# Queries and keys turned by VectorE squares and GpSimd copies; the turned softmax weights stored from ScalarE's queue

## The chip, the cores and the metric

The kernel runs on one core of a Trainium2 chip, in one launch. The metric is the device time of that launch in microseconds (us). A core has TensorE (PE, matrix products, with a weight load PEld of its own in the profile), VectorE (DVE), ScalarE (ACT), GpSimd (POOL) and SyncE (SP), which work through their own instructions in order and wait for each other through semaphores. Transfers are started by an instruction on SP's, ACT's or POOL's queue and run on 16 DMA engines.

## The reference

A decoder trunk of two layers on 256 tokens of 2048 channels, all in float32. Layer one mixes tokens with gated linear attention, layer two with block attention whose block of 256 holds the whole sequence, so that each query sees its own block, causally, with a bias by distance. Each is followed by a gated ConvFFN. The part that the change touches is the second mixer, here for one batch and one block:

```python
q = (rms_norm(x, norm_w) @ w_q).reshape(B, S, H, Dh)          # H = 16 heads of Dh = 128
q = rms_norm(q, q_norm_w) * Dh ** -0.5
k = rms_norm((rms_norm(x, kv_norm) @ w_k).reshape(B, S, H, Dh), k_norm_w)
v = (rms_norm(x, kv_norm) @ w_v).reshape(B, S, H, Dh)
s = einsum('qhd,khd->hqk', q, k) + bias_table[:, rel_bucket(dist)]
p = softmax(where(dist >= 0, s, -inf))
o = einsum('hqk,khd->qhd', p, v)
h = h + o.reshape(B, S, H * Dh) @ w_out
```

## The kernel before

**Weights and steps.** Every weight matrix is streamed from DRAM once, in chunks of 128 x 2048 (1 MB) on SP's queue into three buffers (`wraw`). A chunk is two halves of 1024 columns. ScalarE casts each half to the high part `whi` (L144), VectorE subtracts to get the remainder `wlo` (L146); four buffers of each exist. TensorE multiplies high by high, low by high and high by low parts, which is nearly float32. The Python call `step()` hands out one half and advances a counter `cur`; `after(n, job)` puts a job n steps later, so lags are counted in weight halves. `tc.issue_after(ws.high.ins)` and `ws.low.ins` keep an instruction behind the latest cast on ScalarE, or remainder on VectorE. The final order on each engine is set by a scheduler when the kernel is built; tiles come out of pools, above all 32 slots of 4 KB per partition (`slot`), two PSUM banks for small products (`bank`) and three PSUM accumulators of two banks (`acc`).

**The stage around the change.** `gemm_tok` (L366/L368 belong to its sibling `gemm`, L381/L384 to it) makes four groups of queries, four of keys, four of values, each group four heads of 128 channels with tokens on partitions, in 8 steps of 12 matmuls of 512 columns. Behind each query or key group:

- `head_norm` squares and copies the accumulator out on ScalarE (L989, L990), sums the squares per head on VectorE (L992, L993), raises them to -1/2 on GpSimd (`rr`, L995) and scales the rows on VectorE (L997).
- `features`, two jobs 3 and 4 steps later, turns tokens x channels into channels x tokens: four TensorE transposes of 128 x 128 into a PSUM bank `tr` (L1005), two ScalarE copies out (L1008, L1010) and a VectorE remainder (L1011).
- for keys, `softmax` 5 to 8 steps later: four matmuls per head into `s` (L1021, L1023), bias, minimum, exponential, sum and scaling (L1030 to L1036).
- `turn`, 7 to 10 steps later: VectorE transposes 32 x 32 squares within partitions (L1045); four GpSimd-queue stores to DRAM (L1048) and one load back (L1049) exchange the squares, so that keys lie on partitions.
- `weights`, 15 to 18 steps later: high, low and plain parts on ScalarE and VectorE (L406, L407, L1061).

`values` follows each value group by 1 and 2 steps: eight matmuls per head (L460 to L463) and a split into `ox`, which is what the output projection (`project`, L366/L368) multiplies. `bias_rows` builds the bias rows with a one-hot matmul (L972) and four loads on GpSimd's queue. In the same stage `make_ahead` forms sums of the last weight matrix's blocks on VectorE (L329, L330) and parks them in DRAM (`tsum`, 1 MB each, GpSimd's queue, L339).

`square` (L700) is a helper of the ConvFFN already: after a VectorE transpose of 32 x 32 squares (L722) sixteen GpSimd copies (L705) move the squares between groups of 32 partitions. `turn_h` stores turned squares to DRAM (`hscr`, L874) on SP's queue, 32 KB each.

Of the kernel before, what the change touches and what calls it, by code (L numbers as in the profile page):

```python
# [8 lines left out]
F32 = mybir.dt.float32  # L9
F32R = mybir.dt.float32r  # L10
I32 = mybir.dt.int32
AF = mybir.ActivationFunctionType
OP = mybir.AluOpType
# [5 lines left out]
S = 256  # L19
# [139 lines left out]
def trunk(ctx: ExitStack, tc: tile.TileContext, xT, cst, msk, w1p, w2a, w_k, w_qa, w_v2, w_v, w_g, w_go,  # L159
          w_up0, w_dn0, w_kk, w_kv, w_mq, w_mo, w_up1, w_dn1, rel, onehot, out):  # L160
    nc = tc.nc
    V, A, T = nc.vector, nc.scalar, nc.tensor
# [11 lines left out]
    def slot(shape, dt, name):  # L174
        return big.tile(shape, dt, name=name, tag="slot")

    def temp(name, shape=(128, 2, S), dt=F32):
        return tmp.tile(list(shape), dt, name=name, tag="temp")

    def bank(name, shape):  # L180
        return mis_ps.tile(list(shape), F32, name=name, tag="bank")
# [6 lines left out]
    for layer, todo in enumerate(ahead):  # L188
        t = dram.tile([len(todo), 128, 2048], F32, name=f"tsum{layer}")
# [15 lines left out]
    h = [hs[p // 2][:, p % 2] for p in range(NP)]  # L205
# [4 lines left out]
    kqw = keep.tile([128, 1], F32, name="kqw")  # L210
# [36 lines left out]
    ident = mk[:, 0:128]  # L247
# [73 lines left out]
    def after(steps, job):  # L321
        later.append((cur[0] + steps, job))
# [21 lines left out]
    def after_high():  # L344
        return tc.issue_after(ws.high.ins)

    def after_low():
        return tc.issue_after(ws.low.ins)
# [40 lines left out]
    def rows(xs):  # L389
        return lambda kt: xs[kt // 2][:, kt % 2, :]  # L390

    def both(ps, name):
        t = temp(name)
        A.copy(t, ps[:, :, S:])
        V.tensor_add(t, t, ps[:, :, :S])
        return t
# [8 lines left out]
    def split(dst_hi, dst_lo, src):  # L405
        A.copy(dst_hi, src)  # L406
        V.tensor_sub(dst_lo, src, dst_hi.bitcast(F32))  # L407
# [129 lines left out]
    for hd in range(GH):  # L537
        ps = gemm(xs, KT)
        rstd = nrm.rstd
        k = both(ps, "k")  # L540
        V.tensor_mul(k, k, bc(rstd))
        b = bcum[hd]
        d = small.tile([128, 2, 4], F32, name="dec", bufs=4)
# [63 lines left out]
    for hd in range(GH):  # L607
        ps = gemm(xs, KT)
        q = both(ps, "q")
# [11 lines left out]
    for hd in range(GH):  # L621
        for c in range(2):
            ps = gemm(xs, KT)
            g = both(ps, "g")
# [75 lines left out]
    def square(y, x):  # L700

        for m in range(4):
            xs_ = x[32 * m:32 * m + 32].rearrange("a t (n c b) -> a n t c b", c=4, b=32)
            for c in range(4):
                nc.gpsimd.tensor_copy(y[32 * c:32 * c + 32, :, :, 32 * m:32 * m + 32], xs_[:, :, :, c])  # L705
# [279 lines left out]
    def head_norm(ps, name):  # L985
        t_, sq = slot([128, 2, 512], F32, name), slot([128, 2, 512], F32, "hsq")
        for t in range(2):
            r = n_q.col[:, t:t + 1]
            A.activation(sq[:, t, :], ps[:, t, :], AF.Square, scale=r)  # L989
            A.activation(t_[:, t, :], ps[:, t, :], AF.Copy, scale=r)  # L990
        ss = small.tile([128, 8], F32, name="ss")
        V.tensor_reduce(ss, sq.rearrange("p t (h d) -> p (t h) d", d=128), axis=AX.X, op=OP.add)  # L992
        V.tensor_scalar(ss, ss, 1.0 / 128, EPS, op0=OP.mult, op1=OP.add)  # L993
        rr = small.tile([128, 8], F32, name="rr")
        nc.gpsimd.tensor_tensor(rr, ss, mhalf, op=OP.pow)  # L995
        u = t_.rearrange("p t (h d) -> p (t h) d", d=128)
        V.tensor_mul(u, u, rr[:, :, None].to_broadcast([128, 8, 128]))  # L997
        return t_

    def features(t_, c, f, scale, c0):  # L1000

        tp = bank("tr", (128, 2, S))
        for i in range(2):
            for t in range(2):
                T.transpose(tp[:, i, 128 * t:128 * t + 128],  # L1005
                            t_[:, t, (2 * c + i) * 128:(2 * c + i + 1) * 128], ident)
        whole, halves_ = f[0][:, 2 * c:2 * c + 2, :], f[1][c]
        A.activation(whole, tp[:, :, :128], AF.Copy, scale=scale)  # L1008
        hi, lo = halves_[:, :, 0, :], halves_[:, :, 1, :]
        A.activation(hi, tp[:, :, c0:], AF.Copy, scale=scale)  # L1010
        V.scalar_tensor_tensor(lo, tp[:, :, c0:], scale, hi.bitcast(F32), op0=OP.mult, op1=OP.subtract)  # L1011

    qf, kf, ox = [], [], []
    pts = [None] * MH
    p0s, p1s = [], []

    def softmax(hd):
        (q0, q1), (k0, k1) = qf[hd // 4], kf[hd // 4]
        q1, k1 = q1[hd // 2 % 2][:, hd % 2], k1[hd // 2 % 2][:, hd % 2]
        sp = bank("s", (128, 384))  # L1020
        T.matmul(sp[:, 0:128], q0[:, hd % 4, :], k0[:, hd % 4, :], start=True, stop=True)  # L1021
        for i, (a, b) in enumerate(((0, 0), (0, 1), (1, 0))):
            T.matmul(sp[:, 128:384], q1[:, a, :], k1[:, b, :], start=i == 0, stop=i == 2)  # L1023
        s = temp("s", (128, 384))
        st = small.tile([128, 4], F32, name="st")
        bt = bias[hd // 4][:, hd % 4, :]
        for t, (c0, c1) in enumerate(((0, 128), (128, 384))):
            n = c1 - c0
            rev = bass.AP(tensor=bt.tensor, offset=bt.offset + n - 1, ap=[bt.ap[0], [-1, n]])
            V.tensor_tensor_reduce(s[:, c0:c1], sp[:, c0:c1], rev, -1.0, 3.0e38, OP.add, OP.min,  # L1030
                                   st[:, t:t + 1])
            A.activation(s[:, c0:c1], s[:, c0:c1], AF.Exp, bias=st[:, t:t + 1], scale=-1.0,
                         accum_out=st[:, 2 + t:3 + t])
        V.reciprocal(st[:, 2:4], st[:, 2:4])
        for t, (c0, c1) in enumerate(((0, 128), (128, 384))):
            V.tensor_scalar(s[:, c0:c1], s[:, c0:c1], st[:, 2 + t:3 + t], None, op0=OP.mult)  # L1036
        pts[hd] = s

    turned = dram.tile([MH, 12, 32, 128], F32, name="turned")

    def turn(hd):

        t = slot([128, 2, 384], F32, "pT")
        with tc.issue_after(ws.low.ins):
            V.transpose(t[:, 0], pts[hd])  # L1045
        to = turned[hd].rearrange("f b (m a) -> m b f a", a=32)
        for m in range(4):
            nc.gpsimd.dma_start(to[m], t[32 * m:32 * m + 32, 0].rearrange("b (f a) -> b f a", a=32))  # L1048
        nc.gpsimd.dma_start(t[:, 1].rearrange("k (j q) -> k j q", j=3),  # L1049
                            turned[hd].rearrange("(j f) b q -> (f b) j q", f=4))  # L1050
        pts[hd] = t[:, 1]

    def weights(hd):
        tp = pts[hd]
        if hd % 8 == 0:
            p1s.append(slot([128, 8, 128], F32, "p1"))
        if hd % 2 == 0:
            p0s.append(slot([128, 2, 2, S], F32R, "p0"))
        with tc.issue_after(ws.high.ins):
            split(p0s[-1][:, hd % 2, 0], p0s[-1][:, hd % 2, 1], tp[:, :256])  # L1060
            A.copy(p1s[-1][:, hd % 8], tp[:, 256:])  # L1061
# [17 lines left out]
    for g in range(4):  # L1079
        ps = gemm_tok(xs)  # L1080
        t_ = head_norm(ps, "q")
        if g % 2 == 0:
            q8 = slot([128, 8, 128], F32, "q0")
        q1 = slot([128, 4, 2, 128], F32R, "q1")
        f = (q8[:, g % 2 * 4:g % 2 * 4 + 4], (q1[:, 0:2], q1[:, 2:4]))
        qf.append(f)
        for c in range(2):
            after(3 + c, lambda t_=t_, c=c, f=f: features(t_, c, f, 1.0, 128))
    xs = rows(xkv)
    for g in range(4):  # L1090
        ps = gemm_tok(xs)
        t_ = head_norm(ps, "k")
        if g % 2 == 0:
            k8 = slot([128, 8, 128], F32, "k0")
        f = (k8[:, g % 2 * 4:g % 2 * 4 + 4], [slot([128, 2, 2, S], F32R, f"k1{c}") for c in range(2)])
        kf.append(f)
        for c in range(2):
            after(3 + c, lambda t_=t_, c=c, f=f: features(t_, c, f, kqw, 0))
        for i in range(4):
            after(5 + i, lambda i=i, g=g: softmax(4 * g + i))  # L1100
            after(7 + i, lambda i=i, g=g: turn(4 * g + i))
            after(15 + i, lambda i=i, g=g: weights(4 * g + i))
    for g in range(4):
        ps = gemm_tok(xs)
        if g % 2 == 0:
# [120 lines left out]
```

## Time and profile before

| | us |
|---|---|
| median of 3 runs | 2176.6 (2175.9 to 2176.62) |
| profiled execution | 2175.2 |
| its span, first to last instruction | 2173.4 |
| TensorE's granted clock | 1.000 |
| queries' and keys' transposes on TensorE | 1129.2 to 1310.8 |
| softmax, first score to last weight | 1223 to 1354 |
| last values to the projection | 1384.9 |

Times in the profile count from the span's start. A row of a group names line, engine, operation, output<-input, shapes and count, then its busy time and mean, then the idle time of the engine just before and what ended it. TensorE's matmuls are pipelined, so the duration of one is a latency, and its price is the distance between starts. ScalarE's and VectorE's queues show a DMA start as its own row (`ACTq`, `SPq`), not as busy time; on GpSimd it counts as busy.

### The profile page before, as it was taken

What the parts mean: (1) busy time and instruction counts of PE and PEld (TensorE: products, weight loads), DVE (VectorE), ACT (ScalarE), POOL (GpSimd) and SP (SyncE); (2) the same over time, 40 slices, a digit from 0 to 9 for tenths busy, and PEclk for the clock granted to TensorE, in tenths of its full rate; (3) what the DMA queues carried; (4) which work ended last, traced back from release to release, by engine and by line L of the source; (5) the groups of instructions that cost most, each with busy time, mean ns of one, the idle gap of its engine ahead of it and who ended that gap; (6) DMA issues with size and microseconds to landing.
All of it is one profiled execution on the core that took longest, in us unless ns stands there. A gap on an engine that the chain in (4) does not pass through costs nothing.

```text
span 2173.4 us, 29230 instructions
## 1 busy us (share of the span) xinstructions
PE 2165.5 (100%) x10224; PEld 1815.1 (84%) x10224; DVE 1829.8 (84%) x2531; ACT 1311.9 (60%) x1849; POOL 659.4 (30%) x925
## 2 busy tenths in 40 slices
PE   9999999999999999999999999999999999999999
PEld 7889888888888888887888888888888888888887
DVE  7676877699999897977978787677999999979898
ACT  6655655456565655766756666445565656567575
POOL 0000000264656464300001343003655565542000
PEclk9999999999999999999999999999999999999999
DMA  7575778777778785887967788677787878759896
GB/s 289 209 289 178 263 263 321 287 263 285 273 281 313 275 311 191 329 329 259 366 245 293 275 299 294 228 285 276 284 302 275 310 284 290 293 191 349 325 358 251
DMA packets 113526, 613.01 MB, mean 282 GB/s; under 512 B 29361, under 2 KB 29889, under 8 KB 49634
## 3 DMA queue, kind: packets, MB, share of 16 engines
q1 hardware_dynamic: 94610, 523.75, 66.5%
q0 software_dynamic: 18048, 86.60, 10.5%
q8 instruction: 80, 1.31, 0.2%
q10 hardware_dynamic: 720, 0.79, 0.1%
q14 instruction: 68, 0.56, 0.1%
HBM read 535.31 MB, written 75.78 MB: 281 GB/s over the span
## 4 chain that ended last, share of the span: by engine, by line
PE 98%; DMA 2%; DVE 0%; ACT 0%; issue 0%; ACTq 0%; DVEq 0%; SPq 0%
PE acc L381 40%; PE acc L384 20%; PE acc L803 13%; PE acc L366 11%; PE acc L368 6%; PE p L803 5%; DMA wraw<-w_dn 1%; PE sT L577 0%; DMA sums<-tsum 0%; DMA ahead<-tsum 0%; PE tr L1005 0%; PE s L1023 0%; DVE wlo L146 0%; DMA h<-xT 0%; PE z L483 0%; PE o L463 0%
## 5 line engine op out<-in xcount | busy, mean ns | idle before, releaser
L146 DVE TENSOR_TENSOR wlo<-wraw,whi 128x1024 fp32r<-128x1024 f32 (+1 forms) x788 | 954.3, 1221 | 266.6 <-ACT whi L144 179.8
L144 ACT CAST whi<-wraw 128x1024 fp32r<-128x1024 f32 (+1 forms) x788 | 797.1, 1018 | 611.9 <-PE acc L381 361.8
L381 PE MATMUL acc<-whi,xw 128*128 128x512 f32 x3328 | 825.5, 389 | 0.6 <-DVE xw L261 0.6
L381 PEld LDWEIGHTS acc<-whi,xw 128*128 128x128 f32 x3328 | 623.5, 188 | 130.4 <-issue 1.1
L705 POOL COPY up<-uT 32x256 f32<-32x256 f32 x704 | 520.9, 740 | 310.5 <-DVE uT L722 240.7
L384 PE MATMUL acc<-wlo,xw 128*128 128x512 f32 x1664 | 445.9, 389 | 0.0
L384 PEld LDWEIGHTS acc<-wlo,xw 128*128 128x128 f32 x1664 | 312.1, 188 | 65.0 <-DVE wlo L146 0.3
L339 POOL DMA_DIRECT2D tsum<-ahead x58 | 31.6, 545 | 549.3 <-DVE ahead L330 511.7
L803 PE MATMUL acc<-whi,hid 128*128 128x512 f32 x588 | 168.1, 390 | 1.3 <-ACT whi L144 1.3
L146 DVE TENSOR_TENSOR wlo<-ahead,whi 128x1024 fp32r<-128x1024 f32 x98 | 120.4, 1235 | 19.0 <-ACT whi L144 12.2
L803 PEld LDWEIGHTS acc<-whi,hid 128*128 128x128 f32 x588 | 109.8, 188 | 24.7 <-ACT whi L144 2.3
L381 PE MATMUL acc<-whi,xkv 128*128 128x512 f32 x512 | 129.9, 391 | 0.0
L144 ACT CAST whi<-ahead 128x1024 fp32r<-128x1024 f32 x98 | 101.9, 1054 | 42.9 <-PE p L803 18.5
L366 PE MATMUL acc<-xw,whi 128*128 128x512 f32 x512 | 124.5, 392 | 0.0
L803 PE MATMUL p<-whi,hid 128*128 128x512 f32 x356 | 111.5, 389 | 0.0
L381 PEld LDWEIGHTS acc<-whi,xkv 128*128 128x128 f32 x512 | 95.1, 188 | 18.9
L366 PEld LDWEIGHTS acc<-xw,whi 128*128 128x128 f32 x512 | 93.6, 188 | 17.7
L803 PE MATMUL acc<-whi,comb 128*128 128x512 f32 x348 | 101.3, 390 | 0.7 <-ACT whi L144 0.7
L803 PE MATMUL acc<-wlo,hid 128*128 128x512 f32 x294 | 96.3, 390 | 0.0
L735 ACT ACTIVATE au<-up,cs 128x256 f32<-128x256 f32 x176 | 96.1, 595 | 0.0
L742 DVE SCALAR_TENSOR_TENSOR au<-up,cs,au 128x254 f32<-128x254 f32 x176 | 90.2, 543 | 0.0
L740 DVE SCALAR_TENSOR_TENSOR au<-up,cs,au 128x255 f32<-128x255 f32 x176 | 89.2, 543 | 0.2
(266 smaller groups left out, 2355.3 us busy)
## 6 DMA issues: line engine op xcount, KB each, us to landing
wraw<-w_up SPq DMA_DIRECT2D x176, 1024.0 KB, 5.5
ahead<-w_dn SPq DMA_DIRECT2D x58, 1024.0 KB, 8.9
tsum<-ahead POOLq DMA_DIRECT2D x58, 1024.0 KB, 8.8
ahead<-tsum SPq DMA_DIRECT2D x49, 1024.0 KB, 6.9
wraw<-w_dn SPq DMA_DIRECT2D x58, 768.0 KB, 6.3
wraw<-w_dn SPq DMA_DIRECT2D x30, 1024.0 KB, 6.7
wraw<-w_g SPq DMA_DIRECT2D x16, 1024.0 KB, 4.9
wraw<-w_go SPq DMA_DIRECT2D x16, 1024.0 KB, 6.2
```

What stands on the lines that cost most here:

```text
L144: self.high = nc.scalar.copy(hi[:, a:b], src[:, a:b])
L146: self.low = nc.vector.tensor_sub(lo[:, a:b], src[:, a:b], hi[:, a:b].bitcast(F32))
L339: after(8, lambda: nc.gpsimd.dma_start(parked[layer][at], t))
L366: T.matmul(ps[:, b, :], two[i][0][:, c:c + 128], xs(kt), start=kt == 0, stop=False)
L368: T.matmul(ps[:, b, :S], two[i][1][:, c:c + 128], xs(kt)[:, :S], start=False, stop=kt == kts - 1)
L381: T.matmul(ps[:, t, :], xs(kt)[:, x0 + 128 * t:x0 + 128 * t + 128], hi[:, c:c + 512], start=kt == 0 and x0 == 0, stop=False)
L384: T.matmul(ps[:, t, :], xs(kt)[:, 128 * t:128 * t + 128], lo[:, c:c + 512], start=False, stop=kt == KT - 1)
L705: nc.gpsimd.tensor_copy(y[32 * c:32 * c + 32, :, :, 32 * m:32 * m + 32], xs_[:, :, :, c])
L735: A.activation(au[:, i, :], t[:, i, :], AF.Identity, bias=col(cb + n), scale=col(cw + 2 * 2 * FT + n))
L740: V.scalar_tensor_tensor(au[:, i, 1:], t[:, i, :S - 1], col(cw + 2 * FT + n), au[:, i, 1:], op0=OP.mult, op1=OP.add)
L742: V.scalar_tensor_tensor(au[:, i, 2:], t[:, i, :S - 2], col(cw + n), au[:, i, 2:], op0=OP.mult, op1=OP.add)
L803: T.matmul(p[n], x[xi], w[wi][:, 512 * f:512 * f + 512], start=n not in begun, stop=left[n] == 0)
```

## The change

The four transposes per half group on TensorE and their PSUM bank go. One job per group, 6 steps after it, scales the rows (behind the latest remainder), transposes the 32 x 32 squares of all four heads with one VectorE instruction of 128 x 1024, and lets `square` move them with 16 GpSimd copies into `y`. Two further jobs, 7 and 8 steps after that, read `y` where the PSUM bank was read. The lags of `softmax`, `turn` and `weights` grow from 5, 7, 15 to 17, 19, 30. In `turn`, the four stores move to a job one step later and from GpSimd's queue to ScalarE's, behind the latest cast; the load back stays on GpSimd's queue, in that same job. Line numbers behind the change differ: in the changed kernel the scaling is L1004, the transpose L1005, the copies out L1013, L1014 and L1016, the stores L1059, the load L1060.

```diff
@@ -993,22 +993,30 @@
-        u = t_.rearrange("p t (h d) -> p (t h) d", d=128)
-        V.tensor_mul(u, u, rr[:, :, None].to_broadcast([128, 8, 128]))
-        return t_
-
-    def features(t_, c, f, scale, c0):
-
-        tp = bank("tr", (128, 2, S))
-        for i in range(2):
-            for t in range(2):
-                T.transpose(tp[:, i, 128 * t:128 * t + 128],
-                            t_[:, t, (2 * c + i) * 128:(2 * c + i + 1) * 128], ident)
-        whole, halves_ = f[0][:, 2 * c:2 * c + 2, :], f[1][c]
-        A.activation(whole, tp[:, :, :128], AF.Copy, scale=scale)
-        hi, lo = halves_[:, :, 0, :], halves_[:, :, 1, :]
-        A.activation(hi, tp[:, :, c0:], AF.Copy, scale=scale)
-        V.scalar_tensor_tensor(lo, tp[:, :, c0:], scale, hi.bitcast(F32), op0=OP.mult, op1=OP.subtract)
+        return t_, rr
+
+    def features(t_, f, scale, c0, lag):
+
+        x, y = slot([128, 2, 512], F32, "tr"), slot([128, 4, S], F32, "tr")
+        u, rr = t_
+        u = u.rearrange("p t (h d) -> p (t h) d", d=128)
+        with after_low():
+            V.tensor_mul(u, u, rr[:, :, None].to_broadcast([128, 8, 128]))
+        V.transpose(x.rearrange("p t c -> p (t c)"), t_[0].rearrange("p t c -> p (t c)"))
+        square(y.rearrange("p n (t s) -> p n t s", t=2), x)
+
+        def out_(c):
+            u = y[:, 2 * c:2 * c + 2]
+            whole, halves_ = f[0][:, 2 * c:2 * c + 2, :], f[1][c]
+            hi, lo = halves_[:, :, 0, :], halves_[:, :, 1, :]
+            with after_high():
+                A.activation(whole, u[:, :, :128], AF.Copy, scale=scale)
+                A.activation(hi, u[:, :, c0:], AF.Copy, scale=scale)
+            with after_low():
+                V.scalar_tensor_tensor(lo, u[:, :, c0:], scale, hi.bitcast(F32), op0=OP.mult, op1=OP.subtract)
+
+        for c in range(2):
+            after(lag[c], lambda c=c: out_(c))
@@ -1044,11 +1052,16 @@
         to = turned[hd].rearrange("f b (m a) -> m b f a", a=32)
-        for m in range(4):
-            nc.gpsimd.dma_start(to[m], t[32 * m:32 * m + 32, 0].rearrange("b (f a) -> b f a", a=32))
-        nc.gpsimd.dma_start(t[:, 1].rearrange("k (j q) -> k j q", j=3),
-                            turned[hd].rearrange("(j f) b q -> (f b) j q", f=4))
-        pts[hd] = t[:, 1]
+
+        def store():
+            for m in range(4):
+                with after_high():
+                    A.dma_start(to[m], t[32 * m:32 * m + 32, 0].rearrange("b (f a) -> b f a", a=32))
+            nc.gpsimd.dma_start(t[:, 1].rearrange("k (j q) -> k j q", j=3),
+                                turned[hd].rearrange("(j f) b q -> (f b) j q", f=4))
+            pts[hd] = t[:, 1]
+
+        after(1, store)
@@ -1084,8 +1097,7 @@
-        for c in range(2):
-            after(3 + c, lambda t_=t_, c=c, f=f: features(t_, c, f, 1.0, 128))
+        after(6, lambda t_=t_, f=f: features(t_, f, 1.0, 128, (7, 8)))
@@ -1094,12 +1106,11 @@
-        for c in range(2):
-            after(3 + c, lambda t_=t_, c=c, f=f: features(t_, c, f, kqw, 0))
+        after(6, lambda t_=t_, f=f: features(t_, f, kqw, 0, (7, 8)))
         for i in range(4):
-            after(5 + i, lambda i=i, g=g: softmax(4 * g + i))
-            after(7 + i, lambda i=i, g=g: turn(4 * g + i))
-            after(15 + i, lambda i=i, g=g: weights(4 * g + i))
+            after(17 + i, lambda i=i, g=g: softmax(4 * g + i))
+            after(19 + i, lambda i=i, g=g: turn(4 * g + i))
+            after(30 + i, lambda i=i, g=g: weights(4 * g + i))
```

## The prediction

> **What bounds the kernel now.** I read the page first, then the queries and keys' stage alone: its stretches, its waits, its PE timeline.
>
> ```profile
> PE 2165.5 (100%) x10224; PEld 1815.1 (84%) x10224; DVE 1829.8 (84%) x2531; ACT 1311.9 (60%) x1849; POOL 659.4 (30%) x925
> PE 98%; DMA 2%; DVE 0%; ACT 0%; issue 0%; ACTq 0%; DVEq 0%; SPq 0%
> ...
> 1222.00:1332.00 110.00, 110.00 (x545) 93.06 (x544) 94.79 (x208) 72.78 (x152) 54.47 (x79) 1.00 0.83 290
> 700.00:800.00 100.00, 100.00 (x442) 82.83 (x442) 93.80 (x132) 60.31 (x86) 55.50 (x79) 1.00 0.76 276
> ...
> ACT whi L144 <- PE acc L381: 95.4, 68, 4.4
> ```
>
> The first two rows are the page's busy times and its chain of waits: TensorE is busy for the whole span, and the chain that ends last is TensorE for 98%. The next two are stretches (after the length: PE, PEld, DVE, ACT, POOL busy, granted clock, DMA share): 1222 to 1332 is where the softmax runs, 700 to 800 lies in the first ConvFFN, whose up-projection is turned already in the way that the change brings in. TensorE has no gap in either. The last is the longest of the waits between 1080 and 1400 us: ScalarE's weight cast waits 95.4 us for TensorE to give a weight buffer back; no wait of TensorE for a cast stands in that list. So every TensorE instruction taken out of this stage should come off the end, as long as nothing that replaces it makes TensorE wait.
>
> **What is removed.** 64 transposes of 128x128.
>
> ```profile
> L1005 PE MATMUL tr<-mk,q x32: 270/272/328, 1129.2 to 1195.4; 128*128 128x128 f32 x32
> ...
> L1005 PE MATMUL tr<-mk,k x32: 270/272/273, 1216.2 to 1310.8; 128*128 128x128 f32 x32
> ```
> ```profile
> 1157.96 1.07 PE L384 MATMUL acc<-wlo,xw 128*128 128x512 f32 x4
> 1158.87 1.98 PE L381 MATMUL acc<-whi,xw 128*128 128x512 f32 x8
> 1160.69 1.03 PE L1005 MATMUL tr<-mk,q 128*128 128x128 f32 x8
> 1161.48 1.17 PE L384 MATMUL acc<-wlo,xw 128*128 128x512 f32 x4
> 1162.48 1.98 PE L381 MATMUL acc<-whi,xw 128*128 128x512 f32 x8
> ```
> ```profile
> by line: PE acc L381 61.4%; PE acc L384 30.8%; PE tr L1005 3.6%; PE s L1023 2.5%; PE s L1021 1.5%; PE biasrow L972 0.4%
> ```
>
> The 272 ns are a latency; the price is the distance between starts. Eight L381 matmuls take 1160.69 - 1158.87 = 1.82 us, four L384 matmuls 1158.87 - 1157.96 = 0.91 us; so a weight half (one "step") is 2.73 us. Eight transposes take 1161.48 - 1160.69 = 0.79 us, and the four L384 matmuls behind them 1.00 instead of 0.91. That is 0.88 us per eight, 7.0 us for 64. The chain over 1120 to 1320 us, which holds all 64, says the same: 3.6% of 200 us is 7.2. I take 7.0.
>
> **What is added on VectorE and GpSimd.** Per group of four heads (eight groups) one 128x1024 square transpose on VectorE and 16 copies on GpSimd.
>
> ```profile
> L705 POOL COPY up<-uT 32x256 f32<-32x256 f32 x704 | 520.9, 740 | 310.5 <-DVE uT L722 240.7 <-PE acc L384 22.3 <-issue 20.0
> ...
> L722 DVE STREAM_TRANSPOSE uT<-up 128x512 f32<-128x512 f32 x88 | 58.3, 693 | 0.0
> ...
> L1045 DVE STREAM_TRANSPOSE pT<-s 128x384 f32<-128x384 f32 x16 | 9.0, 571 | 0.2
> ...
> L997 DVE TENSOR_TENSOR k<-k,rr 128x1024 f32<-128x1024 f32 x4 | 4.9, 1221 | 1.6 <-POOL rr L995 1.6
> ```
>
> (Groups by line: busy, mean ns of one | idle before.) From 571 ns at 384 elements and 693 at 512, 1024 come to 693 + 512 x 0.95 = 1180 ns, an estimate; eight are 9.4 us on VectorE, over some 190 us. Its stretch above is 94.79 of 110 busy, and the ConvFFN runs it at 93.80 of 100 with TensorE unbroken, so I price this at 0. The scaling in norm (L997) only moves. ScalarE's and VectorE's copies out read SBUF instead of PSUM; bounded by 0 and by their own length, and off the path, 0.
>
> The 16 copies take 16 x 0.74 = 11.8 us. Behind the scaling and the transpose (1.22 + 1.18) they end 14.2 us after the job starts, and their readers come 7 steps = 19.1 us after it: 4.9 us of cover. GpSimd has 55.5 us free in the softmax stretch, and loses 64 stores of 0.62 us, so it keeps up.
>
> The Trainium skill, "SBUF — State Buffer", section "Who interferes with whom", says that a VectorE instruction with two SBUF inputs and a GpSimd instruction that reads SBUF exclude each other, the later one blocked for the whole of the first. The casts' remainders (L146) are such instructions; by that rule the sum would be that of the fourth rival below. The rows so far don't show VectorE paying:
>
> ```profile
> L705 POOL COPY up<-uT x704: 392/496/1478, 411.6 to 1965.7; 32x256 f32<-32x256 f32 x176
> ...
> L146 DVE TENSOR_TENSOR wlo<-wraw,whi x788: 681/1225/1454, 6.6 to 2161.4; 128x1024 fp32r<-128x1024 f32 x170, 128x512 fp32r<-128x512 f32 x27
> ```
>
> L146's median over all stages, 1225 ns, is that of L997, a like operation in a stage that had no copies (1221); it is the copies that spread, from 392 to 1478.
>
> **What is moved: the stores, to ScalarE's queue.** Here is the risk. ScalarE casts the weights, in order; a store ahead of a cast delays it.
>
> ```profile
> L1048 POOL DMA_DIRECT2D turned<-pT x64: 617/618/682, 1226.9 to 1337.5; - x64
> ...
> its engine sat idle before it (us, times) until:
>   issue: 18.7, 20
> ...
> DMA to landing us min/median/max: 2.0/4.9/10.2
> ```
> ```profile
> L874 SPq DMA_DIRECT2D hscr<-hT x64: 302/450/1941, 1491.3 to 1689.2; - x64
> ```
> ```profile
> turned<-pT POOLq DMA_DIRECT2D x64, 48.0 KB, 4.6
> pT<-turned POOLq DMA_DIRECT2D x16, 192.0 KB, 5.9
> ```
>
> No store of this form on ScalarE is in the trace. The nearest row is hscr on SyncE's queue: 32 partitions to DRAM in pieces of 32 words like these, with 256 pieces where these have 384. Bounds for one: 0.302 and 1.941 us; I take its median, 0.45, so 64 x 0.45 = 28.8 us (by pieces, 0.68 each, 43). ScalarE has 110 - 72.78 = 37.2 us free in the softmax stretch, and the built order of the changed kernel spreads the softmax over a stretch of about that length, with 35 casts from its first to its last store. Beyond that there are the four cast buffers: a cast runs when TensorE frees the buffer of four halves before, so ScalarE may be late by 0.91 + 3 x 2.73 = 9.1 us before TensorE notices. 28.8 against 46.3: price 0. In the built order stores also wait for earlier transfers to land; GpSimd lost 18.7 us in 20 such idle times without a named releaser. With all of these, 47.5 against 46.3, the cover is just gone; I keep that for the second rival.
>
> **What is moved: the later lags.** Softmax comes 12 steps later, weights 15. Early on this is only distance; at the end it meets the output projection.
>
> ```profile
> L1023 PE MATMUL s<-k,q x48: 279/282/364, 1223.1 to 1324.2; 128*128 128x256 f32 x48
> ```
> ```profile
> 1331.73 0.57 DVE L1045 STREAM_TRANSPOSE pT<-s 128x384 f32<-128x384 f32 x1
> ...
> 1353.74 0.42 DVE L407 TENSOR_TENSOR p<-pT,p 128x256 fp32r<-128x256 f32 x1
> ```
> ```profile
> 1384.94 0.12 PE o L460
> ...
> 1392.35 1.91 PE acc L368 x16
> ```
>
> The last head's scores end at 1324.5, its weights are ready at 1354.2, its values run at 1384.9: 30 us of slack. In the built order of the changed kernel only 89 matmuls of 512 columns, 47 of 256 and 4 of 128 stand between the last scores and the first matmul that reads heads 14 and 15: 89 x 0.227 + 47 x 0.119 + 4 x 0.09 = 26.2 us. The chain they must cover: scores to turned block as now, 1332.3 - 1324.2 = 8.1; then on ScalarE a cast and the weights of heads 8 to 11, about 3.0; eight stores 3.6; landing 4.9; load 0.8 and 5.9; cast and remainder 0.8. Sum 27.1: 0.9 us too long, and I take 0.9. With short landings nothing is left; with both at 10.2 it is 27.1 + 5.3 + 4.3 - 26.2 = 10.5. Behind that wait stand the values and then the projection, which reads all heads.
>
> One instruction moves that the change doesn't name: the bias row's matmul stands 41 matmuls after the sum of squares (before: 113 and four transposes), and the one-hot load is issued straight after col_h on GpSimd.
>
> ```profile
> oh<-onehot POOLq DMA_DIRECT2D x1, 48.0 KB, 12.3
> bscr<-brow POOLq DMA_DIRECT2D x1, 24.0 KB, 4.2
> ```
> ```profile
> 1115.06 0.50 PE L307 MATMUL sum_h<-one,acc_sq 128*128 128x1 f32 x4
> ```
> ```profile
> 1116.20 0.71 POOL L315 TENSOR_TENSOR col_h<-mean_h,mhalf 128x2 f32<-128x2 f32 x1 [64.53 <-DVE mean_h L314]
> ...
> 1127.13 0.59 POOL L339 DMA_DIRECT2D tsum<-ahead  x1 [5.14 <-DVE ahead L330]
> 1127.72 0.52 POOL L969 DMA_DIRECT2D oh<-onehot  x1
> ```
>
> It would be issued at 1116.9 and needed at 1115.5 + 41 x 0.227 = 1124.8: 7.9 us. It took 12.3 where a 1 MB store went ahead of it in its queue; now that store is behind it, and the nearest small transfer took 4.2. Price 0, at most 4.4.
>
> **Sum.** 2175.2 (the profiled execution, of which 2173.4 are span) - 7.0 + 0.9 = 2169.1; the runs' median stands 1.4 higher, so 2176.6 - 6.1 = 2170.5.
>
> **Rivals.**
>
> 1. The tail is late: values wait for the last heads' loads, or the one-hot load is late. For it: the slack of 30 us is spent; against it: median landings fit. 2176.6 - 7.0 + 3 to 10 = 2172.6 to 2180, say 2175. Chance 0.14.
>
> 2. ScalarE becomes the bound, between the first scores and the last values: a store costs more than its queue's median, casts fall behind, TensorE waits for whi. It begins at (37.2 + 9.1) / 64 = 0.72 us for one store, and the kernel is slower from (46.3 + 7.0) / 64 = 0.83. At 1.0, about twice my price, 64 - 46.3 = 17.7 are lost: 2176.6 - 7.0 + 17.7 = 2187. For it: the maximum of 1.94, the 0.68 by pieces, the 18.7 us of waits that move along with the stores; against it: the median, and that waits and issue needn't add up, since a landing that is waited for also passes while other stores are issued. Chance 0.18.
>
> 3. The weight stream or an older wait sets the end, and nothing is gained: 2176.6. Against it, the 95.4 us for which casts wait on TensorE. Chance 0.04.
>
> 4. GpSimd's copies block VectorE, casts' remainders come late, TensorE waits for wlo: 128 copies x 0.39 (the shortest) = 50 us, plus 9.4 of transposes; free are 15.2 in 110, so 26 in 190 us, and 9.1 of buffer: 24 us late, 2176.6 - 7.0 + 24 = 2194. For it, the ConvFFN's VectorE at 94%; against it, L146's 1225 ns and TensorE's unbroken 100% there. Chance 0.07. The Trainium skill's rule above is what would bring it about.
>
> **How the numbers follow.** The forecast has 0.57, with its own range 2168.5 to 2172.2. A change under 0.2%, 4.4 us, counts as none. Faster: the forecast's 0.57. Within: rivals 1 and 3, 0.18. Slower: 2 and 4, 0.25. The range begins at 2168.5 (7.2 gained, nothing lost, less the 0.7 by which the runs shown differ) and reaches through rival 1 into the milder half of rival 2, to 2183; left out are the rest of 2 and rival 4.
>
> **What would show it.** Right: no transpose rows on TensorE; its share still 100% in the softmax stretch; the casts still waiting for TensorE; ScalarE's stores at about 0.45 us. Wrong: TensorE waiting for whi or wlo between the first score and the end of the value projection (rival 2, or 4 if L146 grew); a gap before the last o matmuls (rival 1); a gap before the bias row near 1125 us.

## The result and the profile after

| | before | after |
|---|---|---|
| median of 20 runs, us | 2175.96 (2173.74 to 2178.89) | 2179.28 (2175.62 to 2183.57) |
| profiled execution, us | 2175.2 | 2182.57 |
| its span, us | 2173.4 | 2180.8 |
| TensorE's granted clock | 1.000 | 0.996 |

The ratio is 1.0015, with a 95% interval of 1.0009 to 1.0021: the change costs 3.3 us, 0.15%. The granted clock is 0.996 to 0.998 in all 20 runs of the changed kernel, and 0.999 or 1.000 in the runs of the kernel before beside the experiments, so the lower clock of the profiled execution is no accident of that one. The forecast was 2170.5, a gain of 6.1. The time lies inside the range, but on the other side of the starting point from the forecast, so the mechanism has to be found and not only a size.

The page of the changed kernel, busy times and chain of waits:

```profile
PE 2163.9 (99%) x10160; PEld 1812.0 (83%) x10160; DVE 1844.7 (85%) x2539; ACT 1308.3 (60%) x1849; POOL 707.1 (32%) x989
...
PE 95%; DMA 3%; DVE 1%; ACT 1%; issue 0%; ACTq 0%; SPq 0%; DVEq 0%
```

The 64 transposes are gone (10224 matmuls before, 10160 now), yet the chain is TensorE for 95% and no longer for 98%. The stretches tell where it leaves TensorE (PE, PEld, DVE, ACT, POOL busy, granted clock, DMA share); first the kernel before, then the changed one:

```profile
1360.00:1400.00 40.00, 40.00 (x218) 34.74 (x217) 22.62 (x26) 17.67 (x21) 0.56 (x1) 1.00 0.60 211
```
```profile
1222.00:1332.00 110.00, 110.00 (x523) 92.30 (x523) 94.43 (x170) 67.33 (x126) 55.31 (x79) 1.00 0.86 287
...
1360.00:1400.00 40.00, 34.35 (x174) 29.56 (x173) 22.89 (x43) 21.33 (x43) 3.60 (x5) 0.87 0.68 222
```

The softmax stretch, 1222 to 1332, is as it was: TensorE without a gap, VectorE no busier. The loss comes behind it, in the 40 us where the value products meet the output projection: 5.65 us idle, and a clock of 0.87. TensorE's waits and its timeline name what it waits for:

```profile
PE o L460 <- ACT vm L453: 4.8, 1, 4.8
PE acc L803 <- ACT whi L144: 4.0, 3, 2.3
PE o L463 <- ACT vm L456: 1.5, 2, 0.8
```
```profile
1369.65 3.79 PE L366 MATMUL acc<-ox,whi 128*128 128x512 f32 x16
...
1379.82 0.58 PE L460 MATMUL o<-p,vm 128*128 128x256 f32 x1 [4.84 <-ACT vm L453]
...
1383.81 3.66 PE L366 MATMUL acc<-ox,whi 128*128 128x512 f32 x8
1387.31 0.28 PE L460 MATMUL o<-p,vm 128*128 128x256 f32 x1
...
1387.80 0.36 PE L460 MATMUL o<-p,vm 128*128 128x256 f32 x1
```

At 1369.65 the projection begins, before 1377.49: TensorE is 7.8 us ahead, though some of the value products that used to come before it now come after. Then the values of heads 8 to 11 wait for `vm`, ScalarE's copy of their accumulator. After 4.84 us without work, eight L366 matmuls take 1387.31 - 1383.81 = 3.50 us in place of 1.82: half pace. ScalarE's timeline shows why `vm` is late:

```profile
1342.86 5.18 ACTq L1059 DMA_DIRECT2D turned<-pT  x4
...
1357.16 6.10 ACTq L1059 DMA_DIRECT2D turned<-pT  x8
1363.36 0.40 ACT L1040 ACTIVATE s<-s,st 128x128 f32<-128x128 f32 x1 [7.30 <-DMA turned<-pT]
...
1370.88 8.16 ACTq L1059 DMA_DIRECT2D turned<-pT  x8
1379.08 0.69 ACT L453 ACTIVATE vm<-acc,col_h 128x512 fp32r<-128x512 f32 x1 [8.25 <-DMA turned<-pT]
```

The `x4` are the stores of one head, the `x8` those of two. A store isn't counted as busy, but nothing behind it on ScalarE starts until it has been issued: eight hold the engine for 6.1 us, and eight more for 8.2. Behind the second burst stands an exponential of the softmax (L1040), behind the third `vm`. So three bursts within 36 us hold ScalarE for 5.18 + 6.10 + 8.16 = 19.4 us. By the program delay feeds on itself here: the exponentials that stand behind one burst feed the VectorE transposes whose results the next burst stores.

Three starting points of TensorE put sizes to it: the first projection matmuls on `ox`, the last of them, and the last matmuls of the kernel. Here they are in TensorE's timeline of the kernel before, of the changed one (its first is the 1369.65 above), and of a kernel of the experiments below, the changed one with its stores on SyncE's queue:

```profile
1377.49 3.79 PE L366 MATMUL acc<-ox,whi 128*128 128x512 f32 x16
...
1463.27 3.82 PE L366 MATMUL acc<-ox,whi 128*128 128x512 f32 x16
...
2168.89 0.61 PE L803 MATMUL acc<-wlo,hid 128*128 128x512 f32 x2
```
```profile
1466.96 3.82 PE L366 MATMUL acc<-ox,whi 128*128 128x512 f32 x16
...
2176.25 0.61 PE L803 MATMUL acc<-wlo,hid 128*128 128x512 f32 x2
```
```profile
1370.13 3.79 PE L366 MATMUL acc<-ox,whi 128*128 128x512 f32 x16
...
1455.91 3.82 PE L366 MATMUL acc<-ox,whi 128*128 128x512 f32 x16
...
2161.38 0.61 PE L803 MATMUL acc<-wlo,hid 128*128 128x512 f32 x2
```

From the first to the second point the kernel before and the SyncE version both need 85.78 us, the changed one 97.31. That is 11.5 more: 5.65 are gaps; about 2 are the values of four heads, which in the other two traces run ahead of the first point (1387.80 - 1387.31 = 0.5 us a head); and of the rest, nearly 4, the half pace explains 3.3: the clock is at 0.50 for 10.24 us, with 6.58 us of work in them (a row near the end of this text shows it). 0.6 us stay open. From the second to the third point it is 705.6, 709.3 and 705.5 us, in the order of the fences: another 3.7 us are lost in the last stage of this one execution:

```profile
2139.99 0.73 PE L803 MATMUL acc<-whi,hid 128*128 128x512 f32 x2 [2.31 <-ACT whi L144]
```
```profile
2141.57:2144.98 3.41, 3.41 (x10) 2.67 (x9) 3.41 (x4) 3.40 (x5) 0.00 (x0) 0.50 0.69 210
```

A gap of 2.3 us, and a little later 3.41 us at a clock of 0.50, which cost 1.7. The profiled execution stands 3.3 us above the median of the runs; a gap like this one, in some runs and not in others, would account for that, but the other runs have no trace.

### The profile page after: what moved, and what is told of

It reads as the page before. It is cut to its first block, busy times and chain, and to the rows that moved or that the text cites. A ratio compares the mean times of both kernels' runs of the same rounds, so it can differ in the third digit from the quotient of the medians.

```text
span 2180.8 us, 29228 instructions
## 1 busy us (share of the span) xinstructions
PE 2163.9 (99%) x10160; PEld 1812.0 (83%) x10160; DVE 1844.7 (85%) x2539; ACT 1308.3 (60%) x1849; POOL 707.1 (32%) x989
## 4 chain that ended last, share of the span: by engine, by line
PE 95%; DMA 3%; DVE 1%; ACT 1%; issue 0%; ACTq 0%; SPq 0%; DVEq 0%
PE acc L381 39%; PE acc L384 20%; PE acc L803 13%; PE acc L366 11%; PE acc L368 6%; PE p L803 5%; DMA sums<-tsum 1%; DMA wraw<-w_dn 1%; DVE wlo L146 0%; PE sT L577 0%; DMA turned<-pT 0%; DMA ahead<-tsum 0%; DMA wraw<-w_v 0%; ACT whi L144 0%; ACTq L1059 0%
## 5 line engine op out<-in xcount | busy, mean ns | idle before, releaser
L366 PE MATMUL acc<-xw,whi 128*128 128x512 f32 x512 | 124.5, 392 | 0.0
L366 PEld LDWEIGHTS acc<-xw,whi 128*128 128x128 f32 x512 | 93.6, 188 | 17.7
L705 POOL COPY tr<-tr 32x256 f32<-32x256 f32 x128 | 86.6, 677 | 26.8 <-DVE tr L1005 21.8
```

The costliest lines, as they stand in the source:

```text
L366: T.matmul(ps[:, b, :], two[i][0][:, c:c + 128], xs(kt), start=kt == 0, stop=False)
```

## The experiments

The theory after this reading: ScalarE's in-order queue, held by stores, is late with copies that TensorE has no buffer for. Its rivals: (A) the later lags make the last heads' loads late; (B) VectorE's transposes and GpSimd's copies lose the time; (C) the stores cost wherever they stand on ScalarE. Times are medians, ratios are to the kernel before, run on the same chip in the same rounds (its median 2175.8 to 2176.4, a spread of 0.6 us between rounds; the change itself ran in rounds of its own).

### Another queue for the stores

GpSimd's, as before the change:

```diff
-                with after_high():
-                    A.dma_start(to[m], ...)
+                nc.gpsimd.dma_start(to[m], ...)
```

> Theory (ScalarE's order at the tail: eight stores of heads 14 and 15, 8.2 us with their waits for earlier landings, stand ahead of the value copy vm; the 4.8 us gap of TensorE lowers the clock behind it): with the stores on GpSimd's queue vm runs in time, no o matmul waits for vm, the granted clock from 1360 to 1400 is 1.00, and the full gain of the transposes shows: 2176.0 - 7 = 2169, 2168 to 2171. Rival A (the later lags: the last heads' loads come too late whatever queue stores): the o matmuls wait for p, 2173 or more. Rival B (VectorE's transposes and GpSimd's copies lose the time): 2176 or more.

SyncE's:

```diff
-                with after_high():
-                    A.dma_start(to[m], ...)
+                nc.sync.dma_start(to[m], ...)
```

> The changed kernel with the stores on SyncE's queue. Theory: ScalarE is free as with GpSimd, 2169 to 2172, as long as the weight loads that then stand behind waiting stores in SyncE's queue keep one of three buffers ahead. Rival (weight loads come late behind stores that wait for VectorE): casts wait for wraw, TensorE for whi, 2176 to 2186.

GpSimd: 2189.15 us, ratio 1.0058 (1.0045 to 1.0071), the worst of all. SyncE: 2167.69 us, ratio 0.9959 (0.9945 to 0.9972), 8.7 us faster than the kernel before and 11.6 faster than the change. The SyncE version's stretch that was shown above, ScalarE's `vm` for heads 8 to 11, and the stores (minimum, median and maximum in ns; `SPq` is SyncE's queue, not VectorE's); TensorE has no wait at all between 1080 and 1480 us in this trace:

```profile
1360.00:1400.00 40.00, 40.00 (x233) 35.37 (x233) 26.85 (x36) 21.99 (x35) 1.88 (x3) 1.00 0.68 240
```
```profile
1357.17 0.69 ACT L453 ACTIVATE vm<-acc,col_h 128x512 fp32r<-128x512 f32 x1
```
```profile
L1058 SPq DMA_DIRECT2D turned<-pT x64: 302/468/1888, 1260.9 to 1360.7; - x64
```

The same stores take about as long to issue (median 468 ns, 492 on ScalarE), but on a queue that computes nothing. `vm` of heads 8 to 11, at 1379.08 in the change, is at 1357.17. With VectorE's transposes and GpSimd's copies all in place (2539 and 989 instructions, as in the change), rival B falls, and so does rival A for this version. The GpSimd version shows where A does hold (what GpSimd's stores waited for; TensorE's waits; its timeline behind the longest):

```profile
  DVE pT L1053: 21.8, 4
```
```profile
PE o L461 <- DVE p L407: 7.2, 2, 4.8
```
```profile
1379.88 0.58 PE L461 MATMUL o<-p,vm 128*128 128x256 f32 x1 [4.81 <-DVE p L407]
...
1381.70 6.27 PE L366 MATMUL acc<-ox,whi 128*128 128x512 f32 x16
```

There the stores wait 21.8 us in GpSimd's queue for VectorE, and the loads and the next group's copies stand behind them; now `p` is late, TensorE has a gap of nearly the same length, and 16 matmuls take 6.1 us in place of 3.6. This trace is of the slowest of its five runs. My expectation of 2169 for this version was wrong by 20 us: GpSimd had been free enough for the stores only while it had no copies (the kernel with the lags alone, below, has its stores there too, and no such wait).

### The stores alone, the lags alone

The kernel before with its stores on ScalarE, behind the latest cast, and a second one with `nc.sync` in place of `A`; in both the stores and the load back come one step later, as in the change (TensorE's transposes and the old lags stay):

```diff
-            nc.gpsimd.dma_start(to[m], ...)
+            A.dma_start(to[m], ...)
```

> The kernel before with only the four stores per head on ScalarE's queue, one step later; TensorE's transposes and the old lags stay. Theory: the stores are harmful only where a value copy stands right behind them with no buffer left; with the old lags the last stores are 12 steps earlier, the casts' 9.1 us of buffer cover them: 2176 within 2, no wait of an o matmul for vm. Rival C (64 stores on ScalarE cost the path wherever they stand): 3 to 10 us slower than before, 2179 to 2186, with TensorE waiting for whi between 1225 and 1345.

> The kernel before (TensorE's transposes, old lags) with only the stores moved, one step later and to SyncE's queue. Theory (the 8.7 us that the SyncE version of the changed kernel gains are the removed transposes): 2176.4 within 1.5. Rival (the stores' leaving GpSimd is itself worth the 1.7 us above my 7.0, or SyncE's queue as such is the gain): 2174.7 or less.

The kernel before with only the three lags of the change:

```diff
-            after(5 + i, lambda i=i, g=g: softmax(4 * g + i))
-            after(7 + i, lambda i=i, g=g: turn(4 * g + i))
-            after(15 + i, lambda i=i, g=g: weights(4 * g + i))
+            after(17 + i, lambda i=i, g=g: softmax(4 * g + i))
+            after(19 + i, lambda i=i, g=g: turn(4 * g + i))
+            after(30 + i, lambda i=i, g=g: weights(4 * g + i))
```

> The kernel before with only the lags of softmax, turn and weights as in the change (17, 19, 30); transposes on TensorE, stores on GpSimd's queue. Theory: the lags alone leave the last loads just in time, 2176 to 2178. Rival A (the lags make the tail late whatever else): the o matmuls wait for p, 2180 or more.

Stores on ScalarE alone: 2186.18 us, ratio 1.0045 (1.0033 to 1.0058), 10 us slower; I had expected no change. Stores on SyncE alone: 2182.09 us, ratio 1.0026 (1.0016 to 1.0036), where I had also expected none. Lags alone: 2175.36 us, ratio 1.000 (0.9991 to 1.0009), as expected. ScalarE's timeline in the first of these, and TensorE's waits between 1080 and 1480 us:

```profile
1269.23 9.51 ACTq L1051 DMA_DIRECT2D turned<-pT  x7
1278.84 2.95 ACT L144 CAST whi<-wraw 128x1024 fp32r<-128x1024 f32 x3 [8.87 <-DMA turned<-pT]
```
```profile
PE s L1021 <- DVE k L1011: 4.5, 3, 2.5
PE acc L381 <- ACT whi L144: 4.2, 2, 2.1
PE o L462 <- DVE vm L454: 0.9, 1, 0.9
```

One burst holds ScalarE for 9.5 us, which is more than the 9.1 us of cast buffers, and TensorE waits for `whi`. The three waits sum to 9.6 us, nearly all of the loss, at a granted clock of 1.000. So C holds: with the old lags the damage only moves, from `vm` to `whi` and to the turned keys `k`. In the version with stores on SyncE ScalarE waits the other way, for what is loaded back:

```profile
ACT p L406 <- DMA pT<-turned: 17.4, 4, 6.2
ACT p L1065 <- DMA pT<-turned: 14.8, 6, 8.1
```

32 us in all, and ScalarE's casts stand behind these waits; TensorE's own waits there sum to 3.6 of the 6 us lost. The old lag from the stores to `weights` is 7 steps, the change's is 10, and the SyncE version of the change has no such wait: I read the short lag as the cause, though the two kernels differ in the transposes too. By themselves the lags are free.

### Which of the stores, and where

The changed kernel with its stores on two queues. Heads 12 to 15 go to GpSimd's queue here; in the second kernel the condition is `hd >= 14` and the queue `nc.sync`, in the third it is `hd < 14` and `nc.sync`:

```diff
+                if hd >= 12:
+                    nc.gpsimd.dma_start(to[m], ...)
+                    continue
                 with after_high():
                     A.dma_start(to[m], ...)
```

> The changed kernel with the stores of heads 12 to 15 alone on GpSimd's queue, the other 48 on ScalarE's. Theory (the loss is the tail): nearly the whole loss goes, 2169 to 2172, no wait of o for vm. Rival C (the 64 stores cost ScalarE over the whole stretch): a quarter of the 10 us comes back, 2176 to 2178.

> The changed kernel with the eight stores of heads 14 and 15 alone on SyncE's queue, 56 on ScalarE. Theory (the eight that stand ahead of vm are the stall): vm is free of them, no gap of TensorE over 2 us, granted clock 1.00, 2168 to 2172. Rival (pile-up: ScalarE is late already by the stores of heads 8 to 13): vm is late still, 2173 to 2177.

> The reverse: the eight stores of heads 14 and 15 on ScalarE, 56 on SyncE's queue. Theory of place: part of the gap stays, 2170 to 2175, since vm has four stores ahead of it in the built order. Rival of pile-up: ScalarE isn't late when they come, TensorE has no gap over 1 us there, 2167 to 2169.

All stores on ScalarE, but those of heads 14 and 15 three steps later; and all with shorter lags:

```diff
-        after(1, store)
+        after(4 if hd >= 14 else 1, store)
```
```diff
-            after(17 + i, ...softmax...); after(19 + i, ...turn...); after(30 + i, ...weights...)
+            after(15 + i, ...softmax...); after(17 + i, ...turn...); after(26 + i, ...weights...)
```

> The changed kernel with the stores of heads 14 and 15 alone issued 3 steps later; in the built order the value copy vm of heads 8 to 11 then stands behind four of them in place of eight. Theory (vm behind the stores is the stall): o waits about half as long for vm, 2 to 3 us, 2174 to 2177. Rival A (the last heads' loads are what is late): these come up to 8 us later and their o matmuls wait for p, 2180 or more.

> The changed kernel, stores still on ScalarE, with softmax, turn and weights 2, 2 and 4 steps earlier. In the built order the value copy vm of heads 8 to 11 then stands behind fewer of the last stores. Theory (place: what stands behind the last eight stores decides): the 4.8 us wait of o for vm shrinks or goes, 2170 to 2176. Rival C (64 stores hold ScalarE for some 47 us wherever they stand, the old-lag kernel lost 9.7 us by them): 2177 to 2186, with waits of TensorE for whi, k or vm at other places.

The third column is the time in which ScalarE's timeline shows a store being issued, overlaps counted once:

| stores of heads 0 to 13 / 14, 15 | us | ScalarE held, us | ratio (95%) |
|---|---|---|---|
| ScalarE / ScalarE, the change | 2179.28 | 44.5 | 1.0015 (1.0009 to 1.0021) |
| last ones 3 steps later | 2177.36 | 43.5 | 1.0005 (0.9996 to 1.0014) |
| shorter lags | 2176.32 | 46.7 | 1.0006 (0.9997 to 1.0015) |
| ScalarE / SyncE | 2174.16 | 39.6 | 0.9995 (0.9987 to 1.0004) |
| heads 12 to 15 on GpSimd | 2173.86 | 32.3 | 0.9990 (0.9981 to 0.9998) |
| SyncE / ScalarE | 2168.11 | 4.2 | 0.9967 (0.9954 to 0.9979) |
| SyncE / SyncE | 2167.69 | 0 | 0.9959 (0.9945 to 0.9972) |

Taking the last eight away, the very ones ahead of `vm`, recovers 5.1 us, less than half; taking the other 56 away recovers 11.2, nearly all, though the last eight are still on ScalarE. So it isn't the place alone: my expectation for the fourth row (2168 to 2172, "the eight that stand ahead of vm are the stall") fell, and its rival, pile-up, holds. In that version's trace, which is of the slowest of its 11 runs, the bursts of heads 11 to 13 hold ScalarE, and another `vm` is late:

```profile
1344.82 5.89 ACTq L1062 DMA_DIRECT2D turned<-pT  x4
...
1359.83 6.02 ACTq L1062 DMA_DIRECT2D turned<-pT  x8
```
```profile
1352.44 0.79 PE L463 MATMUL o<-p,vm 128*128 128x128 f32 x2 [2.82 <-ACT vm L456]
```

In the reverse the last eight come in time and in two short bursts, which hold it for 1.9 us from 1351.39 and for 2.3 us from 1358.80; TensorE has no gap over 1 us there, and the expectation by pile-up, 2167 to 2169, holds.

The second and third rows are in between: a better order shortens the waits and leaves the load. None of the expectations for rows two, three and five came out. With the last stores three steps later I expected half the wait and 2174 to 2177; the waits for `vm` went only from 6.3 to 4.7 us, and the time is 2177.36. The shorter lags landed between their two ranges (2170 to 2176 and 2177 or more). With heads 12 to 15 on GpSimd the time lies between 2169 to 2172 and 2176 to 2178, and a wait of 2.6 us for `vm` is left where the theory of the tail had none.

### What makes a store long

Two kernels that leave the turn out, so that a store writes few long pieces; with four stores per head and with one:

```diff
+            flat = turned[hd].rearrange("f b q -> (f b q)").rearrange("(p x) -> p x", x=384)
-                    A.dma_start(to[m], t[32 * m:32 * m + 32, 0].rearrange("b (f a) -> b f a", a=32))
+                    A.dma_start(flat[32 * m:32 * m + 32], t[32 * m:32 * m + 32, 0])
```
```diff
-            for m in range(4):
-                with after_high():
-                    A.dma_start(to[m], ...)
+            with after_high():
+                A.dma_start(flat, t[:, 0])
```

> The changed kernel with each of the 64 stores on ScalarE writing 32 pieces of 1536 B in place of 384 of 128 B; what is read back is then not the turned block (the turn is left out), the waits and the bytes are the same. Theory L (a store is held until the transfer eight before it has landed, whatever its own pieces): the stores' rows on ScalarE still sum to 35 us or more with single ones over 2 us, time 2175 to 2180. Rival P (the pieces set the time of a store, 0.45 us and more): the sum falls to about 64 x 0.31 = 20 us, vm is not held, 2168 to 2171.

> The changed kernel with one flat store per head on ScalarE (128 pieces of 1536 B, 16 stores in all; what is read back isn't the turned block). The 64 flat stores held ScalarE 36.1 us, the 64 of the change 44.5. Theory L (most of a store's time is the wait for the transfer eight before): 16 stores on ScalarE have few transfers to wait for, sum 16 x 0.31 to 16 x 0.8 = 5 to 13 us, 2167 to 2169. Rival (a store's time goes with what it writes, 0.56 us per 32 partitions): sum about 36 us again, 2169 to 2172.

64 flat stores: 2170.59 us, ratio 0.9976 (0.9968 to 0.9985), ScalarE held for 36.1 us. 16 flat stores: 2167.88 us, ratio 0.9965 (0.9951 to 0.9979), held for 7.9 us. Their rows beside that of the change (minimum, median and maximum in ns):

```profile
L1059 ACTq DMA_DIRECT2D turned<-pT x64: 309/492/3394, 1261.7 to 1378.6; - x64
...
DMA to landing us min/median/max: 1.6/4.4/8.7
```
```profile
L1060 ACTq DMA_DIRECT2D turned<-pT x64: 308/437/1797, 1261.5 to 1371.0; - x64
```
```profile
L1059 ACTq DMA_DIRECT2D turned<-pT x16: 326/326/1267, 1261.1 to 1359.3; - x16
```

A twelfth of the pieces takes 8.4 of 44.5 us off; a quarter of the instructions, for the same bytes, takes 28 of the remaining 36. The number of transfers started in a burst is what is paid for, more than what they carry. For the first of these neither theory came out whole: the sum of 36 us is the one that theory L expected, but no store took over 2 us, and the time is the rival's 2168 to 2171, with 36 us spread more evenly. For the second, theory L's sum and time hold and the rival's sum does not.

The reason that theory L gives does not hold, though. In the built order each store waits for one of eight completion counters, which SyncE's and ScalarE's transfers take in turn, so that a store waits for the transfer eight before it. For the longest store of the change that is the store that started at 1333.83 (its row and landing; the long one; the stretch that it falls in, with the DMA share last but one):

```profile
L1059 ACTq DMA_DIRECT2D turned<-pT x1: 480/480/480, 1333.8 to 1333.8; - x1
...
DMA to landing us min/median/max: 3.0/3.0/3.0
```
```profile
1344.65 3.39 ACTq L1059 DMA_DIRECT2D turned<-pT  x1
```
```profile
1342.90:1348.00 5.10, 5.10 (x28) 4.36 (x28) 3.10 (x6) 0.14 (x2) 0.00 (x0) 1.00 0.97 385
```

It had landed at 1336.8, 7.8 us before the long store began, so the counter held nothing. The DMA engines were 97% busy meanwhile, and the four stores of that burst landed 8.0 to 8.7 us after their issue, twice the median. That points to full DMA engines behind the long single stores; it is read from one moment of one trace, and no run tests it.

## Why the prediction was wrong, point by point

- **64 transposes, -7.0 us: right.** The kernel before and the SyncE version need the same 85.78 us from the first to the second starting point above, and the first comes at 1377.49 and at 1370.13, 7.4 us earlier. Their medians differ by 8.7; where the rest comes from stays open. From the kernel with the lags alone the spans go from 2172.1 to 2165.9 us, 6.2 less.
- **VectorE's transposes and GpSimd's copies, 0: right for TensorE.** A transpose took 1235 ns (estimated 1180); the SyncE version has them all and no wait of TensorE in the stage. Rival 4 did not occur, but the reading that VectorE doesn't pay was wrong. The median over all stages, 1225 ns, hid it. By stage the remainders' means are these: the kernel before from 1120 to 1370 us, where it has no copies, and from 700 to 860, where it has; then the changed kernel from 1120 to 1370.

```profile
L146 DVE TENSOR_TENSOR wlo<-wraw,whi 128x1024 fp32r<-128x1024 f32 x84 | 102.2, 1222 | 43.3 <-ACT whi L144 38.7 <-PE acc L384 4.1
...
L146 DVE TENSOR_TENSOR wlo<-wraw,whi 128x1024 fp32r<-128x1024 f32 x59 | 78.1, 1324 | 16.9 <-ACT whi L144 16.8
```
```profile
L146 DVE TENSOR_TENSOR wlo<-wraw,whi 128x1024 fp32r<-128x1024 f32 x85 | 106.7, 1260 | 38.6 <-ACT whi L144 37.9
```

  The Trainium skill, "SBUF — State Buffer", section "Who interferes with whom", would have these instructions and GpSimd's reads lock each other out. The stages agree with it in direction: where there are copies the mean is 1324 and 1260 in place of 1222. In the change that is 85 x 38 ns, some 3 us of VectorE (an estimate), for which no TensorE instruction waited.
- **The stores, priced at 0: the step that failed.** It was "28.8 against 46.3: price 0", and both halves of it were off. The price of one store was taken from a median, 0.45 us. The median came out near that, 0.49, but what ScalarE loses is the sum: 44.5 us, 0.70 a store, with single ones of up to 3.4. The nearest row had warned of it with its maximum of 1.94, and the sum by pieces, 43, which stood beside it, came near by luck: with a twelfth of the pieces the stores still held ScalarE for 36.1 us. The larger error is the cover. 37.2 us free in the stretch and 9.1 us of cast buffers were added up as if any idle moment could hide any store. By that comparison even 44.5 us would have cost nothing, against 46.3. But the last three bursts took 5.2, 6.1 and 8.2 us, and in an in-order queue a burst is hidden only by the slack of the next instruction behind it. The casts have 9.1 us of it, by the estimate; `vm` and the exponentials, which stand behind two of these bursts, had too little, as the 4.84 us wait shows.
- **Rival 2 named the mechanism** (ScalarE late because of the stores, between the first scores and the last values) but not how it shows: it put the point from which the kernel is slower at 0.83 us a store, and it looked for waits for `whi`. At 0.70 the kernel is slower already, by waits for `vm`. Its chance of 0.18 was too low for a step that the text itself called the risk.
- **The tail, +0.9: wrong place.** That chain ran from the last scores over stores and loads to the last heads' weights. Its eight stores, put at 3.6 us, took 8.2. The loads were in time in the change all the same; `vm` of an earlier group of heads was not, and it did not stand in the chain that I wrote down, because I followed the data of the moved step and not the queue it moved into. Where the loads do come late, in the GpSimd version, it cost 2189.15.
- **The bias row, 0: right.** No wait of TensorE near 1125 us is in the trace after.

So the change gains what was predicted and loses some 11 us to one of its parts, the choice of ScalarE for the stores. On SyncE's queue the same change is 8.7 us faster than the kernel before.

## What to carry to other kernels

Price a DMA start on a computing engine by the sum over its rows, waits for issue included, and compare each burst with the slack of the very next instruction behind it in that engine's order; free time elsewhere in the stretch doesn't count. When a step moves to another queue, list what stands behind it there, and who waits for that, before following its own data. A queue that only issues transfers can bear waiting stores, if its loads run far enough ahead and the reader's lag is long enough.

## What the runs showed of the hardware that was not expected

**Issue time adds up.** The Trainium skill, "DMA: Bandwidth & Descriptors", section "Issuing engines are not separate DMA queues", says that starting transfers from several engines saves only the sequencer's time to start them, usually little beside the transfer. For a single store these runs agree: 0.70 us of ScalarE beside a landing of 4.4 us in the median. But 64 of them hold a computing engine for 44.5 us, and 11.6 us of the kernel lie between two choices of the queue.

**What a gap costs depends on where it falls.** After gaps of 4.84 us (the change), 4.81 (stores on GpSimd), 2.82 (heads 14 and 15 on SyncE) and 2.31 us (the last stage of the change), matmuls ran at half pace. After 2.63 us (heads 12 to 15 on GpSimd) and 2.46 us (only the stores moved to ScalarE) they did not. In these traces the granted clock changes only at points of a grid of 3.41 us, and the half pace lasts one, two or three steps of it. Here are the steps around the gap of 4.84 us, and two steps over the gap of 2.63 us (TensorE's busy time behind the length, the granted clock third from the end):

```profile
1373.57:1376.98 3.41, 1.42 (x12) 1.21 (x11) 0.02 (x1) 0.00 (x0) 0.00 (x0) 1.00 0.99 350
1376.98:1387.22 10.24, 6.58 (x21) 5.62 (x22) 5.61 (x7) 5.28 (x8) 1.51 (x2) 0.50 0.74 215
```
```profile
1345.31:1348.72 3.41, 1.73 (x8) 1.08 (x7) 0.06 (x1) 0.74 (x1) 0.00 (x0) 1.00 1.01 423
1348.72:1352.14 3.42, 2.47 (x14) 2.21 (x15) 3.08 (x7) 1.84 (x4) 0.00 (x0) 1.00 0.96 259
```

The second gap straddles a point of the grid, so that TensorE works for half of either step, or more. The busy times are the profile's, which models the ends of matmuls. Over the 14 traces, from the first full clock to 2155 us, nine steps at full clock had 1.76 us or more idle, and the half clock followed all nine; 51 had 0.5 to 1.75 us idle, and it followed one, with 1.61. So about half a step idle costs the clock. The Trainium skill, "TensorE: Matmul & The Clock Gate", section "What's actually happening", gives the half clock to a window of about 3.4 us of idleness and says that the window runs freely. The length agrees with the grid; a window that is idle throughout wasn't needed here.
